# Merged rows of the last branch added by transfers on POOL's queue, their parts one chunk later; T1's product written third

## The chip, the cores and the metric

The kernel runs on one core of one Trainium2 chip. The metric is the device time of one execution in microseconds (us). Of the kernel before, three runs gave a median of 1742.87 us, from 1741.56 to 1743.77. The engines are named as the profile names them: PE multiplies matrices, ACT and DVE work on tiles elementwise, POOL also computes and issues transfers (DMAs), and SP issues transfers only.

## The reference

The kernel computes one layer of an encoder: three token mixers run side by side, each is projected by its own matrix `w_branch`, the three results are gated and summed to `merged`, and `merged` is multiplied by `w_out` and added to x. A feed-forward part follows. The part that matters here, cut from the reference:

```python
branches = jnp.stack([s5_out, diff_out.astype(x.dtype), mem_out.astype(x.dtype)], axis=2)
br = jnp.einsum('blnc,ncd->blnd', branches, w_branch[li])
gates = jax.nn.sigmoid((gl + b_gate[li]).astype(F32)).reshape(Bsz, L, N_BRANCH, D_MODEL)
merged = jnp.sum(gates * br.astype(F32), axis=2).astype(x.dtype)
x = x + merged @ w_out[li]
```

There are 768 tokens in all (256 of one request, 512 of another), and D_MODEL is 1024.

## The kernel before

**Parts.** Every dense product is made of three matmuls (`mm3`, lines 755 to 757): both operands are split into a high part, which is a rounded copy (made by ACT), and a low part, which is the remainder (made by DVE), and hi·hi, hi·lo and lo·hi are added up in one accumulator. So each tile of weights costs ACT one copy and DVE one subtraction before PE can use it.

**Weights.** SP loads raw weights (`wr`, line 539, three buffers of 512 KB). A plain tile becomes `wh` (ACT, line 599) and `wl` (DVE, line 605; in an earlier stage an accumulating transfer of 512 KB, line 603, adds the raw weights onto the negated high part). Each of `wh` and `wl` has four buffers.

**The last branch.** The function `branch7` multiplies the second token mixer's output (n_ = 1) by its 1024 x 1024 matrix in four chunks c of 256 output columns. Each chunk works on two by two blocks, where A are the weights' blocks and B the tokens' blocks, and needs seven products of blocks in place of eight: A11·B11, A12·B21, S2·T2, S1·T1, S3·T3, A22·T4 and S4·B22. S1 to S4 are sums of A blocks, which POOL makes (lines 574, 575, 581 and 583, into `ws`). Their parts, and those of the A blocks, come from lines 557 (ACT, high) and 558 (DVE, low); in the trace a pair is called `wh_A`, `wl_A`, `wh_S` or `wl_S` by the first block in the tile. T1 to T4 are sums of B blocks, made earlier; `ra` holds B11 and B21, `rb` holds B22 and T1, `rc` holds T2 and T3, and `mgd` holds T4. One product is 4 steps of k with three matmuls of 128x384, so 12 matmuls, and a chunk is 84.

**Accumulators.** A11·B11, S2·T2 and S3·T3 add onto one accumulator after another (`brc` in the trace, `chain` in the code), and between them ACT copies its value out: to c11 after the first (line 1683), c12 after the second (line 1685), and c21 after the third (line 1690). S1·T1 has an accumulator of its own (`br`), which is copied to c22 (line 1687) and on which S4·B22 then goes on. A12·B21 and A22·T4 have one each. DVE adds accumulators to c11, c12, c21 and c22 (line 1673). c11 and c12 are the two halves of the first staging tile `bs`, c21 and c22 those of the second. Staging tiles come from a pool of two buffers, so a chunk's first copy into each waits until the chunk before is done with it.

**Merge.** For each of the chunk's two rows m of 128 columns by 768 tokens, POOL loads the gate's logits (`glr`, line 1657, 384 KB, two buffers) and ACT makes the tanh (line 1658). DVE multiplies gate and staging tile in place (line 1677), the row of `merged` is increased by it (line 1678, on POOL for m = 0 and on DVE for m = 1), and ACT and DVE make the sum's high and low part in `mgd` (lines 1679 and 1680). All of this belongs to `merge(m)`.

**After the branch.** `out_rows` multiplies `mgd` by `w_out` (`wo` in the trace) in two halves of four rows, the second half needing rows 4 to 7, and adds x (line 1730). x is loaded by POOL (line 1707) into the buffer that `rc` had.

**Order.** Each engine runs its instructions in a fixed order, which a scheduler sets when the program is built; it may put an instruction ahead of one that the code has earlier, so that chunk 3's A11·B11, for one, stands among chunk 2's products. Engines wait for each other by semaphores, and a waiting instruction holds all behind it on its engine.

Of the kernel before, what the change touches and what calls it, by code (L numbers as in the profile page):

```python
# [8 lines left out]
F32 = mybir.dt.float32  # L9
# [621 lines left out]
def hybrid_block(ctx, tc, A, outs, consts):  # L631
# [866 lines left out]
    with ExitStack() as c5:  # L1498
# [146 lines left out]
        MG = rows_pair("mgd", 0)  # L1645
        RB["T4"] = tuple(t[:, 6:8].rearrange("p a (b t) -> p (a b) t", b=2) for t in MG)

        def branch7(n_):
            for c in range(4):
                w = W.get()  # L1650
# [13 lines left out]
                def prod(l, r, ps=None, start=True):  # L1664
                    if ps is None:
                        ps = psd("br")[:, 0:HT]
                    (wh, wl), (xh, xl) = w[l], RB[r]
                    for k in range(4):
                        mm3(ps, wh[:, k], wl[:, k], xh[:, k], xl[:, k], start and k == 0, k == 3, not start)
                    return ps  # L1670
# [4 lines left out]
                def merge(m):  # L1675
                    M = 2 * c + m
                    v.scalar_tensor_tensor(out=cs[m], in0=gs[m], scalar=1.0, in1=cs[m], op0=add, op1=mul)
                    (v if m else gp).tensor_tensor(out=merged[:, M], in0=merged[:, M], in1=cs[m], op=add)
                    act.activation(MG[0][:, M], merged[:, M], AF.Copy, scale=0.5)
                    v.scalar_tensor_tensor(out=MG[1][:, M], in0=merged[:, M], scalar=0.5,  # L1680
                                           in1=MG[0][:, M].bitcast(F32), op0=mul, op1=sub)

                act.activation(c11, prod("A11", "B11", chain), AF.Copy)
                plus(c11, prod("A12", "B21"))
                act.activation(c12, prod("S2", "T2", chain, False), AF.Copy)
                p5 = prod("S1", "T1")
                act.activation(c22, p5, AF.Copy)
                prod("S3", "T3", chain, False)
                plus(c22, chain)
                act.activation(c21, chain, AF.Copy)  # L1690
                if c < 3:
                    plus(c12, prod("S4", "B22", p5, False))
                    merge(0)
                    plus(c21, prod("A22", "T4"))
                    merge(1)
                else:
                    plus(c21, prod("A22", "T4"))
                    merge(1)
                    plus(c12, prod("S4", "B22", p5, False))
                    merge(0)  # L1700
# [335 lines left out]
```

## Time and profile before

| What | Time |
|---|---|
| Profiled execution | 1743.06 us |
| Its span, first to last instruction | 1741.3 us |
| PE, DVE, ACT, POOL busy in it | 1726.6, 1300.5, 908.6, 302.5 us |
| Last branch's first matmul starts | 1120.74 us after the span's start |
| First matmul of the output product starts | 1183.75 us |

The page of the profile gives the busy time of each engine over the whole span. A timeline gives each instruction's start and duration in us, its engine, its line, what it writes and reads (buffer numbers left out), and in brackets how long the engine stood idle before it and whose instruction ended that. PE's matmuls overlap, so the distance between starts is their pace, and it is shorter than one's duration. The row of a stretch (`a:b`) gives busy times of the engines, and near its end the granted clock of PE, 1.00 being full speed. Rows of transfers give the time that the issue took, and from issue to landing.

### The profile page before, as it was taken

To read this page: it belongs to the slowest core of one execution; us is meant where nothing else is said; L and a number is where in the kernel's file an instruction comes from. 1 tells how busy PE (TensorE), PEld (TensorE's weight loads), DVE (VectorE), ACT (ScalarE), POOL (GpSimd) and SP (SyncE) were. 2 spreads that over 40 slices of the span, in tenths; PEclk is the share of its full clock that TensorE was granted. 3 is DMA by queue.
4 is the path that set the end of the run, shared out by engine and by line. 5 is a ranking of instruction groups with operands and counts; after the bars stand their busy time and mean duration, and the time that the engine had idled before them with its cause. 6 is when DMAs were issued, how large, how long until landed. Compare 5 with 4: busy or idle time off the path is not lost.

```text
span 1741.3 us, 29531 instructions
## 1 busy us (share of the span) xinstructions
PE 1726.6 (99%) x11188; PEld 1608.1 (92%) x11188; DVE 1300.5 (75%) x2405; ACT 908.6 (52%) x1924; POOL 302.5 (17%) x308
## 2 busy tenths in 40 slices
PE   9999999999999999999999999999999999999999
PEld 9999988999999999999989888998889999998887
DVE  7665749699999778887886536685598777776775
ACT  7444543776767346877765434353343333334443
POOL 0000000000000100111000001341036555541130
PEclk9999999999999999999999999999999999999999
DMA  7222636755556454745653435335312323239974
GB/s 268 78 85 91 125 120 135 186 125 143 145 159 159 115 140 103 164 91 156 155 165 117 140 116 157 103 111 174 97 55 91 110 91 109 92 110 295 248 157 97
DMA packets 209213, 234.09 MB, mean 134 GB/s; under 512 B 57832, under 2 KB 173296, under 8 KB 209072
## 3 DMA queue, kind: packets, MB, share of 16 engines
q1 hardware_dynamic: 182160, 167.49, 32.0%
q0 software_dynamic: 17440, 58.34, 15.6%
q10 hardware_dynamic: 9472, 6.39, 1.3%
q8 instruction: 88, 1.44, 0.4%
q14 instruction: 53, 0.43, 0.1%
HBM read 165.78 MB, written 41.22 MB: 119 GB/s over the span
## 4 chain that ended last, share of the span: by engine, by line
PE 95%; DVE 2%; ACT 1%; issue 0%; DMA 0%; POOL 0%; SPq 0%; ACTq 0%; DVEq 0%
PE gl L755 4%; PE gl L756 4%; PE gl L757 4%; PE gate L755 3%; PE gate L756 3%; PE up L756 3%; PE gate L757 3%; PE up L755 3%; PE up L757 3%; PE dn L757 3%; PE dn L755 3%; PE dn L756 3%; PE br L755 3%; PE br L757 3%; PE br L756 3%; PE qk L755 3%
## 5 line engine op out<-in xcount | busy, mean ns | idle before, releaser
L599 ACT ACTIVATE wh<-wr 128x1024 fp32r<-128x1024 f32 x116 | 131.9, 1138 | 52.3 <-PE br L756 13.3
L605 DVE TENSOR_TENSOR wl<-wr,wh 128x1024 fp32r<-128x1024 f32 x74 | 99.2, 1342 | 63.5 <-ACT wh L599 61.7
L755 PE MATMUL gl<-H,wh 128*128 128x256 f32 (+1 forms) x384 | 132.2, 344 | 0.0
L757 PE MATMUL gl<-H,wl 128*128 128x256 f32 (+1 forms) x384 | 129.0, 336 | 0.0
L756 PE MATMUL gl<-H,wh 128*128 128x256 f32 (+1 forms) x384 | 128.7, 335 | 0.0
L603 POOL DMA_DIRECT2D wl<-wr x42 | 36.6, 872 | 483.3 <-ACT wl L602 464.1
L755 PE MATMUL qk<-wh,H 128*128 128x256 f32 x384 | 108.3, 282 | 0.0
L756 PE MATMUL qk<-wl,H 128*128 128x256 f32 x384 | 108.0, 281 | 0.0
L757 PE MATMUL qk<-wh,H 128*128 128x256 f32 x384 | 107.3, 279 | 0.0
L558 DVE TENSOR_TENSOR wl_S<-ws,wh_S 128x512 fp32r<-128x512 f32 x84 | 70.7, 863 | 26.2 <-ACT wh_S L557 26.2
L756 PE MATMUL dn<-wld,dxh 128*128 128x512 f32 x231 | 89.6, 389 | 0.0
L755 PE MATMUL dn<-whd,dxh 128*128 128x512 f32 x231 | 89.5, 389 | 0.0
L757 PE MATMUL dn<-whd,dxl 128*128 128x512 f32 x231 | 88.9, 389 | 0.0
L557 ACT ACTIVATE wh_S<-ws 128x512 fp32r<-128x512 f32 x84 | 49.5, 625 | 73.5 <-PE up L756 36.6
L757 PEld LDWEIGHTS gl<-H,wl 128*128 128x128 f32 x384 | 72.0, 188 | 8.1
L756 PEld LDWEIGHTS gl<-H,wh 128*128 128x128 f32 x384 | 72.2, 188 | 7.2
L755 PEld LDWEIGHTS gl<-H,wh 128*128 128x128 f32 x384 | 72.3, 188 | 6.9
L757 PEld LDWEIGHTS qk<-wh,H 128*128 128x128 f32 x384 | 72.6, 189 | 0.6
L755 PEld LDWEIGHTS qk<-wh,H 128*128 128x128 f32 x384 | 72.4, 188 | 0.6
L756 PEld LDWEIGHTS qk<-wl,H 128*128 128x128 f32 x384 | 72.3, 188 | 0.5
L1296 DVE TENSOR_REDUCE nm<-sc 128x1 f32<-128x512 f32 (+1 forms) x96 | 56.7, 597 | 18.1 <-PE sc L1291 17.2
L1298 ACT ACTIVATE p<-sc,nm 128x512 f32<-128x512 f32 (+1 forms) x96 | 58.8, 615 | 14.4 <-DVE nm L1296 13.9
(535 smaller groups left out, 6076.2 us busy)
## 6 DMA issues: line engine op xcount, KB each, us to landing
wr<-in_w_in_dram SPq DMA_DIRECT2D x48, 512.0 KB, 5.0
wr<-in_w_gate_up_dram SPq DMA_DIRECT2D x44, 512.0 KB, 3.6
wl<-wr POOLq DMA_DIRECT2D x42, 512.0 KB, 5.4
wr<-in_w_branch_dram SPq DMA_DIRECT2D x24, 512.0 KB, 4.5
glr<-gl_scr POOLq DMA_DIRECT2D x24, 384.0 KB, 3.5
hid_scr<-fa SPq DMA_DIRECT2D x11, 768.0 KB, 6.4
wr<-in_w_mem_kv_dram SPq DMA_DIRECT2D x16, 512.0 KB, 4.4
wr<-in_w_in_dram SPq DMA_DIRECT2D x32, 256.0 KB, 3.9
```

Source lines behind the costliest of these rows:

```text
L557: self.nc.scalar.activation(f(hi), src, AF.Copy)
L558: self.nc.vector.tensor_tensor(out=f(lo), in0=src, in1=f(hi).bitcast(F32), op=ALU.subtract)
L599: self.nc.scalar.activation(hi, r, AF.Copy)
L603: self.nc.gpsimd.dma_start(lo, r.bitcast(F32R), accum_op=ALU.add)
L605: self.sub.tensor_tensor(out=lo, in0=r, in1=hi.bitcast(F32), op=ALU.subtract)
L755: pe.matmul(ps, wh, xh, start=start, stop=False, **kw)
L756: pe.matmul(ps, wh, xl, start=False, stop=False, **kw)
L757: pe.matmul(ps, wl, xh, start=False, stop=stop, **kw)
L1296: v.tensor_reduce(out=nm[:, m : m + 1], in_=ps, axis=AX.X, op=ALU.max, negate=True)
L1298: act.activation(pm[:, 0:n], ps, AF.Exp, bias=nm[:, m : m + 1], accum_out=s1s[:, tt : tt + 1] if m == 0 else s2)
```

## The change

In chunks 0 to 2, `merge` no longer adds the gated row with DVE or POOL; a transfer on POOL's queue adds the staging tile to the row of `merged` in memory (line 1684 now). The parts of these rows move into a function of their own (lines 1649 and 1650), which is called in the next chunk, after the copy to c21. In chunk 3 the addition is on DVE for both rows (line 1686), with the parts at once. The product S1·T1 and its copy stand before S2·T2 in the code. The gated product stays on DVE (line 1682), and other lines only shift: 1673 is now 1678, the copies to c11, c22, c12 and c21 are lines 1689, 1692, 1693 and 1696, the gate's two lines are 1662 and 1663, x's load is 1716 and its addition 1739.

```diff
@@ -1645,6 +1645,11 @@
+        def merged_parts(M):
+            act.activation(MG[0][:, M], merged[:, M], AF.Copy, scale=0.5)
+            v.scalar_tensor_tensor(out=MG[1][:, M], in0=merged[:, M], scalar=0.5,
+                                   in1=MG[0][:, M].bitcast(F32), op0=mul, op1=sub)
+
         def branch7(n_):
@@ -1675,19 +1680,23 @@
                 def merge(m):
                     M = 2 * c + m
                     v.scalar_tensor_tensor(out=cs[m], in0=gs[m], scalar=1.0, in1=cs[m], op0=add, op1=mul)
-                    (v if m else gp).tensor_tensor(out=merged[:, M], in0=merged[:, M], in1=cs[m], op=add)
-                    act.activation(MG[0][:, M], merged[:, M], AF.Copy, scale=0.5)
-                    v.scalar_tensor_tensor(out=MG[1][:, M], in0=merged[:, M], scalar=0.5,
-                                           in1=MG[0][:, M].bitcast(F32), op0=mul, op1=sub)
+                    if c < 3:
+                        gp.dma_start(merged[:, M], cs[m], accum_op=add)
+                    else:
+                        v.tensor_tensor(out=merged[:, M], in0=merged[:, M], in1=cs[m], op=add)
+                        merged_parts(M)
 
                 act.activation(c11, prod("A11", "B11", chain), AF.Copy)
                 plus(c11, prod("A12", "B21"))
-                act.activation(c12, prod("S2", "T2", chain, False), AF.Copy)
                 p5 = prod("S1", "T1")
                 act.activation(c22, p5, AF.Copy)
+                act.activation(c12, prod("S2", "T2", chain, False), AF.Copy)
                 prod("S3", "T3", chain, False)
                 plus(c22, chain)
                 act.activation(c21, chain, AF.Copy)
+                if c:
+                    for m in range(2):
+                        merged_parts(2 * c - 2 + m)
                 if c < 3:
                     plus(c12, prod("S4", "B22", p5, False))
                     merge(0)
```

What the scheduler makes of it is shown at three places. First POOL, from the first row's merge of chunk 1 to the last gate load of the branch. Before (`merged<-merged,bs` is the addition, `ws` the weights' sums, `glr` a gate load; numbers tell buffers apart):

```order
L1678 TENSOR_TENSOR merged<-merged,bs_13786 128x768
L574 TENSOR_TENSOR ws_13896<-wr_0_13625,wr_1_13747 128x512
L1657 DMA glr_13923<-gl_scr_152 128x768
L575 TENSOR_TENSOR ws_13897<-ws_13896,wr_0_13625 128x512
L1657 DMA glr_13926<-gl_scr_153 128x768
L583 TENSOR_TENSOR ws_13897<-wr_1_13747,ws_13897 128x512
L581 TENSOR_TENSOR ws_13910<-wr_0_13625 128x512
L1678 TENSOR_TENSOR merged<-merged,bs_13929 128x768
L1657 DMA glr_14047<-gl_scr_154 128x768
L1657 DMA glr_14050<-gl_scr_155 128x768
```

And now, where `DMA merged<-bs` is the accumulating transfer:

```order
L1684 DMA merged<-bs_13782 128x768
L1662 DMA glr_13919<-gl_scr_152 128x768
L574 TENSOR_TENSOR ws_13892<-wr_0_13625,wr_1_13743 128x512
L575 TENSOR_TENSOR ws_13893<-ws_13892,wr_0_13625 128x512
L1684 DMA merged<-bs_13783 128x768
L1662 DMA glr_13922<-gl_scr_153 128x768
L583 TENSOR_TENSOR ws_13893<-wr_1_13743,ws_13893 128x512
L581 TENSOR_TENSOR ws_13906<-wr_0_13625 128x512
L1684 DMA merged<-bs_13925 128x768
L1662 DMA glr_14043<-gl_scr_154 128x768
L1684 DMA merged<-bs_13926 128x768
L1662 DMA glr_14046<-gl_scr_155 128x768
```

Where one addition stood per chunk, two transfers stand now in chunks 1 and 2, each ahead of a gate load; the sums of lines 574 and 575 follow each other with no gate load between, the transfer of chunk 1's second row stands behind them, and chunk 3's addition has left POOL.

Second ACT, from the last weight sum's copy of chunk 3's weights to the second gate of chunk 3. `bs<-brc` and `bs<-br` are the copies of accumulators, `mgd<-merged` the high part of a merged row, line 599 a weight copy for the output product. Before:

```order
L557 ACTIVATE wh_S_13906<-ws_13910 128x512
L599 ACTIVATE wh_0_14035<-wr_0_13778 128x1024
L1690 ACTIVATE bs_13930<-brc_13931 128x384
L1679 ACTIVATE mgd<-merged 128x768
L1683 ACTIVATE bs_14053<-brc_14055 128x384
L1658 ACTIVATE glr_14047<-glr_14047 128x768
L599 ACTIVATE wh_1_14041<-wr_1_13892 128x1024
L1685 ACTIVATE bs_14053<-brc_14055 128x384
L1679 ACTIVATE mgd<-merged 128x768
L1687 ACTIVATE bs_14054<-br_14096 128x384
L1658 ACTIVATE glr_14050<-glr_14050 128x768
```

And now:

```order
L557 ACTIVATE wh_S_13902<-ws_13906 128x512
L599 ACTIVATE wh_0_14031<-wr_0_13774 128x1024
L1696 ACTIVATE bs_13926<-brc_13927 128x384
L1689 ACTIVATE bs_14049<-brc_14051 128x384
L1649 ACTIVATE mgd<-merged 128x768
L1663 ACTIVATE glr_14043<-glr_14043 128x768
L599 ACTIVATE wh_1_14037<-wr_1_13888 128x1024
L1693 ACTIVATE bs_14049<-brc_14051 128x384
L1692 ACTIVATE bs_14050<-br_14079 128x384
L1649 ACTIVATE mgd<-merged 128x768
L1663 ACTIVATE glr_14046<-glr_14046 128x768
```

The high part of chunk 2's first row (before line 1679, now 1649) stood ahead of chunk 3's copy to c11 and now stands behind it; the copy to c22 moves ahead of the second row's high part.

Third PE, in chunk 3, the last four matmuls ahead of S3·T3 and its first two (`br<-mgd` is A22·T4, `brc<-rc,wh_A` S2·T2, `brc<-rc,wh_S` S3·T3). Before:

```order
L757 MATMUL br_14124<-mgd,wl_S_13916 128x384
L755 MATMUL br_14124<-mgd,wh_S_13915 128x384
L756 MATMUL br_14124<-mgd,wh_S_13915 128x384
L757 MATMUL br_14124<-mgd,wl_S_13916 128x384
L755 MATMUL brc_14055<-rc,wh_S_13906 128x384
L756 MATMUL brc_14055<-rc,wh_S_13906 128x384
```

And now:

```order
L757 MATMUL brc_14051<-rc,wl_A_13897 128x384
L755 MATMUL brc_14051<-rc,wh_A_13896 128x384
L756 MATMUL brc_14051<-rc,wh_A_13896 128x384
L757 MATMUL brc_14051<-rc,wl_A_13897 128x384
L755 MATMUL brc_14051<-rc,wh_S_13902 128x384
L756 MATMUL brc_14051<-rc,wh_S_13902 128x384
```

In chunk 3 the products ran S1·T1, S2·T2, A22·T4, S3·T3, S4·B22, and now run S1·T1, A22·T4, S2·T2, S3·T3, S4·B22, so that S3·T3 follows S2·T2 at once on the same accumulator. In the order before, S1·T1 already stood third in all four chunks, ahead of S2·T2.

## The prediction

> **What bounds the kernel now.** I read the page first, then the list of waits of PE (TensorE's matmuls), and then, for the stretch that the change touches, the timeline of each engine.
>
> ```profile
> span 1741.3 us, 29531 instructions
> ...
> PE 1726.6 (99%) x11188; PEld 1608.1 (92%) x11188; DVE 1300.5 (75%) x2405; ACT 908.6 (52%) x1924; POOL 302.5 (17%) x308
> ...
> PEclk9999999999999999999999999999999999999999
> ...
> PE brc L757 <- DVE wl_A L558: 2.1, 1, 2.1
> PE av L1327 <- ACT aT L1315: 1.6, 2, 1.2
> ```
>
> PE is busy for 99% of the span at full granted clock, so this change can win only what PE loses in its own stretch. The second part says where PE waits: its longest wait of the whole run, 2.1 us, is for line 558 on DVE, inside the last branch. The timeline of PE shows the branch from its first matmul to the first of the output product (wo):
>
> ```profile
> 1120.74 0.34 PE L755 MATMUL brc<-ra,wh_A 128*128 128x384 f32 x1
> ...
> 1126.99 0.33 PE L755 MATMUL br<-mgd,wh_A 128*128 128x384 f32 x1
> ...
> 1156.28 0.34 PE L756 MATMUL brc<-ra,wh_A 128*128 128x384 f32 x1
> 1158.74 0.44 PE L757 MATMUL brc<-ra,wl_A 128*128 128x384 f32 x1 [2.12 <-DVE wl_A L558]
> ...
> 1160.17 0.52 PE L755 MATMUL brc<-ra,wh_A 128*128 128x384 f32 x1
> ...
> 1163.36 0.34 PE L756 MATMUL brc<-rc,wh_S 128*128 128x384 f32 x1
> ...
> 1175.12 0.45 PE L755 MATMUL brc<-rc,wh_A 128*128 128x384 f32 x1 [0.33 <-ACT bs L1683]
> ...
> 1183.75 0.39 PE L755 MATMUL wo<-wh,mgd 128*128 128x512 f32 x1
> ```
>
> From 1120.74 to 1126.99 stand 36 matmuls, so one takes 0.1736 us. The branch has 4 chunks of 7 products of 12, 336 matmuls, worth 58.33 us: at that pace it would end at 1179.07. It ends at 1183.75. I call the difference PE's lag; at the end it is 4.68 us, and that is all that can be won. It arises at three places: the wait before 1158.74 (1158.74 less 1156.28 less one pitch, 2.29), ten matmuls 0.32 apart from 1160.17 to 1163.36 (3.19 less 1.74, 1.45), and about 0.5 at 1175.12. The second is the granted clock. In a row by stretch it is the third number from the end, here of this branch, and below it of an earlier stage:
>
> ```profile
> 1160.00:1162.00 2.00, 2.00 (x8) 2.00 (x7) 2.00 (x3) 0.63 (x1) 0.32 (x1) 0.50 0.62 219
> ...
> 905.00:910.00 5.00, 3.58 (x21) 1.00 0.00 0
> ```
>
> After the wait of 2.1 us the clock was 0.50 and the matmuls crept till 1163.36. Between 905 and 910 us PE was idle for 1.42 of 5 us, after a wait of up to 1.2 (L1327), and the clock stayed at 1.00.
>
> What makes the first wait is seen on DVE and POOL:
>
> ```profile
> 1137.84 2.33 DVE L558 TENSOR_TENSOR wl_S<-wr,wh_S 128x512 fp32r<-128x512 f32 x1
> 1141.92 0.95 DVE L1677 SCALAR_TENSOR_TENSOR bs<-glr,bs 128x768 f32<-128x768 f32 x1
> 1155.15 3.54 DVE L558 TENSOR_TENSOR wl_A<-wr,wh_A 128x512 fp32r<-128x512 f32 x2
> 1160.44 0.94 DVE L1677 SCALAR_TENSOR_TENSOR bs<-glr,bs 128x768 f32<-128x768 f32 x1
> 1169.75 0.68 DVE L558 TENSOR_TENSOR wl_S<-ws,wh_S 128x512 fp32r<-128x512 f32 x1
> 1186.04 1.22 DVE L605 TENSOR_TENSOR wl<-wr,wh 128x1024 fp32r<-128x1024 f32 x1
> ...
> 1137.32 2.30 POOL L1678 TENSOR_TENSOR merged<-merged,bs 128x768 f32<-128x768 f32 x1
> 1154.24 2.22 POOL L1678 TENSOR_TENSOR merged<-merged,bs 128x768 f32<-128x768 f32 x1 [2.34 <-DVE bs L1677]
> 1156.42 1.71 POOL L574 TENSOR_TENSOR ws<-wr,wr 128x512 f32<-128x512 f32 x1
> 1158.08 0.55 POOL L1657 DMA_DIRECT2D glr<-gl_scr  x1
> 1158.66 1.30 POOL L575 TENSOR_TENSOR ws<-ws,wr 128x512 f32<-128x512 f32 x1
> ```
>
> An L558 subtraction that nothing disturbs takes 0.68 us (1169.75). The one at 1137.84 began while POOL added merged rows and took 2.33, ending when POOL had ended and 0.55 more had passed; the pair at 1155.15 took 3.54, one ending after POOL's addition, the other after its L574. So an operation of DVE on two SBUF inputs and one of POOL exclude each other here. POOL's addition of 1154.24 costs DVE some 2.2 us, and PE waits for that.
>
> **The change, part by part.** Terms are in lag at the end of the branch; positions are counted in matmuls from 1120.74.
>
> *POOL's and DVE's additions of chunks 0 to 2 go* (three at 2.22 to 2.30 or 1.84 us on POOL, three at 0.95 on DVE), and the scheduler puts the weight work where they were. With DVE's pair of 1155.15 at its undisturbed pace (2 x 0.62) PE finds its weights at matmul 206. The wait of 2.29 goes, the slow clock behind it too: lag there 0 instead of 3.7.
>
> *Six accumulating transfers come in.* Before shows no such transfer from `bs` to `merged`; the nearest are the weight remainders (L603, the first pair of rows), also added into SBUF, and the plain gate loads of 384 KB (L1657, the row between); the last pair is the weight loads:
>
> ```profile
> L603 POOL DMA_DIRECT2D wl<-wr x42: 850/857/1007, 294.7 to 1252.7; - x42
> ...
> DMA to landing us min/median/max: 4.5/5.4/9.5
> ...
> DMA to landing us min/median/max: 3.1/3.4/4.2
> ...
> L539 SPq DMA_DIRECT2D wr<-in_w_branch_dram x3: 367/368/368, 1132.4 to 1151.9; - x3
> ...
> DMA to landing us min/median/max: 3.5/3.7/4.1
> ```
>
> The issue of an L603 holds POOL for 0.86 us, against 2.2 for the addition. Landing, from the start of the issue: at least 3.1 (the fastest gate load, same bytes, but plain), at most 5.4 (the median of L603, which moves 512 KB). L603 undisturbed takes 4.5, and these have 3/4 of its bytes but share the rings with the gate load that follows at once and with weight loads; I take 4.4, nearest to L603. The Trainium skill (DMA: Bandwidth & Descriptors, "Anatomy of one DMA — SWDGE (gpsimd) path") fits a POOL transfer by 2.0 us plus its bytes at 436 GB/s: 2.9 us by estimate for 384 KB. By it the lags below would nearly all vanish; for 512 KB it gives 3.2 where L603 shows 4.5 to 9.5, so I follow the rows.
>
> The transfer still reads `bs` when it is in flight, and the staging tiles have two buffers: a chunk's first copy into `bs` (ACT L1683 and L1687, now L1689 and L1692) waits for the landing of the chunk before. Behind these copies ACT holds the weight splits, and PE's chain products wait for the copies themselves. Before, the same place was:
>
> ```profile
> 1170.93 0.96 DVE L1677 SCALAR_TENSOR_TENSOR bs<-glr,bs 128x768 f32<-128x768 f32 x1
> 1171.97 1.84 POOL L1678 TENSOR_TENSOR merged<-merged,bs 128x768 f32<-128x768 f32 x1 [3.29 <-DVE bs L1677]
> 1173.85 0.85 ACT L1679 ACTIVATE mgd<-merged 128x768 fp32r<-128x768 f32 x1 [0.36 <-POOL merged L1678]
> 1174.60 0.47 ACT L1683 ACTIVATE bs<-brc 128x384 f32<-128x384 f32 x1
> ...
> 1146.46 0.47 ACT L1687 ACTIVATE bs<-br 128x384 f32<-128x384 f32 x1
> ...
> 1147.56 1.14 ACT L557 ACTIVATE wh_S<-ws 128x512 fp32r<-128x512 f32 x2
> ...
> L1673 DVE TENSOR_TENSOR bs<-bs,br x12: 537/542/556, 1127.4 to 1184.7; 128x384 f32<-128x384 f32 x12
> ```
>
> From the gated product (L1677) to the next chunk's first copy went 1.84 + 0.85 + 0.47 us with small gaps: 1170.93 + 0.96 to 1175.07, 3.2. Now it is 4.4 + 0.47 and a signal or two, 5.0. Link by link:
>
> 1. Second row of chunk 0: L1677 started at 1141.92 before, 0.95 long. POOL no longer holds DVE at 1137.84 (2.33 to 0.68), so it ends near 1141.6. Landing 1146.0, copy 1146.5 instead of 1146.93; with the parts (0.75) and the gate (0.75) behind it, ACT's splits start 1147.9 against 1147.56. About even.
> 2. Second row of chunk 1: DVE is ahead, but POOL's two sums L574 and L575 now follow each other without an issue between. L574 needs the weight load issued near 1152.2, which lands 3.7 to 4.1 later, so the sums run 1156.3 to 1159.4, and the gated product behind the second ends at 1160.35 (started 1160.44 before). Landing 1164.75, copy of c22 1165.3. PE's S4·B22 of chunk 2, matmul 246, is due at 1163.45: lag 1.85.
> 3. The same landing frees ACT's part (ends 1166.0), DVE's (0.95), then four weight subtractions of 0.62 with a wait of about 1.3 among them for ACT's split and POOL's L581 (to 1170.8), then two additions (0.47, 0.55): 1171.8. On the last waits S1·T1 of chunk 3, since its accumulator is the one S4·B22 used: matmul 276, due 1168.65, lag 3.1. Two matmuls of S4·B22 now stand behind S3·T3; they end before 1170, ahead of DVE.
> 4. A22·T4 (matmul 288, due 1170.74) waits for the accumulator that DVE frees after the gated product (0.95), a weight remainder (1.14, the pitch of 1186.04) and an addition (0.55): 1174.4, lag 3.65.
> 5. First row of chunk 2: gated product 1171.8 to 1172.75, landing 1177.15, copy 1177.65. S2·T2 of chunk 3 is matmul 300 now, due 1172.82: lag 4.9. A22·T4 ahead of it covers 2.08 us, which is already in the count.
> 6. S3·T3 follows S2·T2 at once in chunk 3 and adds onto the same accumulator, so it waits for the copy of c12: 0.33 for the last matmul, some 0.75 left of the weight copy ahead of it on ACT (1.05), 0.47. Another 1.5: lag 6.4. Before, A22·T4 stood between and covered it.
>
> So 6.4 against 4.68: +1.7. The weight loads share the rings with the new transfers; if the load of link 2 takes 4.1 to 4.5, links 2 to 6 move by up to 0.8; I add 0.5. Sum: +2.2.
>
> *T1's product third*: the order of before already has it third in all four chunks, so the rewritten line alone gives 0; what moves is A22·T4 of chunk 3 (links 5 and 6).
>
> *The last chunk's additions both on DVE, its order of products, and the x loads:*
>
> ```profile
> 1189.91 2.67 DVE L1680 SCALAR_TENSOR_TENSOR mgd<-merged,mgd 128x768 fp32r<-128x768 f32 x2 [0.91 <-ACT mgd L1679]
> ...
> 1197.59 0.69 DVE L1730 TENSOR_TENSOR x<-x,wo 128x512 f32<-128x512 f32 x1 [5.01 <-PE wo L757]
> ```
>
> The output product first needs the last two rows' parts in its second half, and x after that. The parts end at 1192.58 before and near 1194 now; PE reaches that half 52 matmuls in, near 1196 before and 1198 now: 0, covered by 4 us. The loads of x, behind POOL's addition till 1190.65, move up to about 1183.5; first used at 1197.59, behind PE: 0.
>
> **Sum.** The profiled execution took 1743.06 us (span 1741.3), 0.19 above the median 1742.87 of the three runs. 1743.06 + 2.2 = 1745.3.
>
> **The rivals.**
>
> *Short landing.* Three landings lie in series (links 1, 2 and 5). If the transfers land like the fastest gate load, in 3.1, that is 3 x 1.3 less: lag 3.0 with the loads' 0.5, so 1741.4, and 1740.9 if the loads are not disturbed. For it speaks the size; against it every L603. Chance 0.14. By the Trainium skill's fit (same page and section) the same sum comes to 1740.8, an estimate.
>
> *Long landing: slower.* ACT's queue becomes the bound. The place is the copies behind links 1, 2 and 5; a landing of 4.85 decides, from where three times the excess (0.45) carries the change past +3.5. At the median of L603, 5.4, lag is 6.9 + 3.0: 1748.3. For it speaks that median, which is what such transfers took with loads beside them; against it 3/4 of the bytes. Chance 0.30.
>
> *The clock drops again.* The new waits are 0.5 to 1.9 us each, between the 1.2 that left the clock at 1.00 and the 2.12 that halved it. If the one of link 2 halves it for 3.3 us, at most 1.45 is added: 1746.7. The Trainium skill (TensorE: Matmul & The Clock Gate, Part 1, the HAM clock gate) lets the clock drop after an idle window of about 3.4 us, and by that rule nothing is added; the trace has it drop after 2.12 us of waiting. Chance 0.10, counted as slower.
>
> *Faster by more than 3.5* would need landings shorter than any shown and link 6 hidden too: 0.04.
>
> **How the numbers follow.** A measurement here can tell about 0.2%, 3.5 us, from no change: 1739.4 to 1746.4. My forecast, 3.7 to 4.85 us of landing, has 0.42 and lies within; short landing lies within as well. Faster 0.04, same 0.56, slower 0.40. The forecast's own range is 1743.2 to 1746.6. The range for 8 in 10 runs from the short landing (1740.9) to one of 5.4 with a slow clock (1748.3 + 1.45, 1749.8).
>
> **What the profile of after would show.** Right: no wait at the third matmul of chunk 3's first product; landings of 4 to 5 us for `merged<-bs`; PE's waits named to ACT's copies into `bs` (S4·B22 of chunk 2, S2·T2 and S3·T3 of chunk 3) and to DVE's addition before chunk 3's T1 product; ACT idle until a transfer ahead of L1689 and L1692; the first wo matmul near 1186. Wrong: landings outside 3.1 to 5.4, PE still waiting for an L558, or PE's waits gone while the branch ends as late.

## The result: slower by 0.26%, within the range

The changed kernel took 1746.89 us (median of 10 runs, 1745.27 to 1749.84) against 1742.83 of the kernel before in its 10 runs beside it: a ratio of 1.0026, with a 95% interval of 1.0016 to 1.0036, or 4.06 us more. The prediction said 1745.3 in a range of 1740.9 to 1749.8. The time lies within that range, but 0.3 us above the forecast's own narrower range (1743.2 to 1746.6) and above 1746.4, up to which the prediction counted a time as no change.

The page of the changed kernel's profile, its first lines:

```profile
span 1744.9 us, 29543 instructions
PE 1725.3 (99%) x11188; PEld 1605.8 (92%) x11188; DVE 1294.9 (74%) x2403; ACT 909.1 (52%) x1924; POOL 298.8 (17%) x310
```

PE is busy about as long as before (1726.6 us then) and DVE 5.6 us less; what grew is PE's waiting. The list of PE's waits (line waited for, total us, times, longest):

```profile
PE brc L755 <- ACT bs L1689: 2.7, 2, 1.8
PE brc L755 <- ACT bs L1693: 2.3, 1, 2.3
...
PE br L755 <- ACT bs L1692: 1.2, 1, 1.2
PE br L755 <- DVE bs L1678: 1.1, 2, 0.9
```

The wait for line 558 is gone, and six waits in its own stretch stand in its place, all for ACT's copies out of accumulators and for DVE's additions behind them. PE's timeline shows where:

```profile
1118.54 0.34 PE L755 MATMUL brc<-ra,wh_A 128*128 128x384 f32 x1
...
1157.42 0.44 PE L755 MATMUL brc<-rc,wh_S 128*128 128x384 f32 x1 [0.91 <-ACT bs L1689]
...
1163.74 0.44 PE L755 MATMUL br<-rb,wh_S 128*128 128x384 f32 x1 [1.16 <-ACT bs L1692]
...
1170.12 0.44 PE L755 MATMUL br<-rb,wh_S 128*128 128x384 f32 x1 [0.91 <-DVE bs L1678]
...
1172.71 0.45 PE L755 MATMUL br<-mgd,wh_S 128*128 128x384 f32 x1 [0.23 <-DVE bs L1678]
...
1176.92 0.44 PE L755 MATMUL brc<-rc,wh_A 128*128 128x384 f32 x1 [1.83 <-ACT bs L1689]
...
1181.54 0.44 PE L755 MATMUL brc<-rc,wh_S 128*128 128x384 f32 x1 [2.26 <-ACT bs L1693]
...
1187.38 0.39 PE L755 MATMUL wo<-wh,mgd 128*128 128x512 f32 x1
```

The branch now takes 1187.38 - 1118.54 = 68.84 us against 63.01 before, so the lag at its end (over 336 matmuls at 0.1736, 58.33 us) is 10.51 against 4.68: 5.83 us more. The span grew by 3.6 only, since the branch began 2.20 us earlier in this execution. In the profiles shown below the branch, whose code ahead is the same in all of them, begins anywhere from 1118.5 to 1121.6, so that part is taken as the difference of one execution from another; from the branch's end to the end of the span it is 557.5 us in both. The lag tells more than the span of one profile, and the medians of the runs decide on the time.

Why the copies come late is seen in chunk 3. The group of the accumulating transfers, whose last line is the least, median and greatest us from issue to landing:

```profile
L1684 POOL DMA_DIRECT2D merged<-bs x6: 865/878/908, 1135.2 to 1174.0; - x6
...
DMA to landing us min/median/max: 4.3/4.8/7.1
```

The same line of the group of this branch's gate loads:

```profile
DMA to landing us min/median/max: 3.4/5.2/7.6
```

POOL's timeline, the issues of chunk 2's transfers and chunk 3's first gate load:

```profile
1171.36 0.88 POOL L1684 DMA_DIRECT2D merged<-bs  x1 [3.98 <-DVE bs L1682]
1171.95 0.87 POOL L1662 DMA_DIRECT2D glr<-gl_scr  x1
1173.95 0.86 POOL L1684 DMA_DIRECT2D merged<-bs  x1 [1.14 <-DVE bs L1682]
```

And ACT's timeline:

```profile
1176.38 0.49 ACT L1689 ACTIVATE bs<-brc 128x384 f32<-128x384 f32 x1 [6.25 <-DMA merged<-bs]
...
1179.32 0.84 ACT L1663 ACTIVATE glr<-glr 128x768 f32<-128x768 f32 x1 [1.72 <-DMA glr<-gl_scr]
1180.07 1.04 ACT L599 ACTIVATE wh<-wr 128x1024 fp32r<-128x1024 f32 x1
1181.01 0.47 ACT L1693 ACTIVATE bs<-brc 128x384 f32<-128x384 f32 x1
```

The first row's transfer of chunk 2 is issued at 1171.36; ACT's copy to c11 waits for its landing till 1176.38, 6.25 us idle. The gate load issued right behind it, at 1171.95, lands at 1179.3; before the change gate loads took 3.1 to 4.2. ACT's tanh (L1663) waits for it another 1.72, a weight copy follows, and only then the copy to c12 (L1693), for which S3·T3 waits. After that wait of 2.26 the clock dropped. Of the rows by stretch, the last shows it (0.57, the third number from the end). The two ahead of it show how full the 16 DMA engines were (the second number from the end, 1 being all busy; in these rows it comes out a little above 1 at times):

```profile
1176.00:1178.00 2.00, 1.08 (x6) 1.00 0.99 355
1178.00:1180.00 2.00, 1.27 (x8) 1.00 1.10 246
...
1182.00:1184.00 2.00, 2.00 (x9) 0.57 0.13 35
```

### The profile page after: what moved, and what is told of

It reads as the page before. It is cut to its first block, busy times and chain, and to the rows that moved or that the text cites. A ratio compares the mean times of both kernels' runs of the same rounds, so it can differ in the third digit from the quotient of the medians.

```text
span 1744.9 us, 29543 instructions
## 1 busy us (share of the span) xinstructions
PE 1725.3 (99%) x11188; PEld 1605.8 (92%) x11188; DVE 1294.9 (74%) x2403; ACT 909.1 (52%) x1924; POOL 298.8 (17%) x310
## 4 chain that ended last, share of the span: by engine, by line
PE 96%; DVE 1%; ACT 1%; DMA 1%; issue 0%; SPq 0%; POOL 0%; ACTq 0%
PE gl L755 4%; PE gl L757 4%; PE gl L756 4%; PE gate L755 3%; PE gate L757 3%; PE gate L756 3%; PE up L757 3%; PE up L756 3%; PE up L755 3%; PE br L756 3%; PE dn L757 3%; PE br L757 3%; PE br L755 3%; PE dn L755 3%; PE dn L756 3%; PE qk L756 3%
```

## The experiments

In the kernels below, unless said otherwise, each engine's order in the branch is pinned row by row to that of the kernel named, by an order-only edge between neighbours, since the scheduler would answer any edit with an order of its own. So an edit shows alone. Only t1_alone stands as the scheduler built it. Each ratio is against runs of the kernel before made beside that kernel; their medians lay between 1741.93 and 1742.83, so rows compare better by ratio than by median. The lags are of one profiled execution each. The numbers of all:

| Kernel | Additions of chunks 0 to 2 | Lag at branch's end, us | Median, us | Ratio to before, 95% interval |
|---|---|---|---|---|
| before | POOL and DVE | 4.68 | 1742.83 | |
| t1_alone | POOL and DVE | 4.98 | 1743.24 | 1.0004 (0.9994 to 1.0013) |
| before_dve | DVE | 2.36 | 1739.85 | 0.9986 (0.9977 to 0.9995) |
| late_parts_dve | DVE | 3.68 | 1740.83 | 0.9991 (0.9982 to 1.0000) |
| dve_order_back | DVE | 1.15 | 1738.59 | 0.9981 (0.9972 to 0.9990) |
| changed kernel | transfers | 10.51 | 1746.89 | 1.0026 (1.0016 to 1.0036) |
| plain_transfer | transfers that don't add | 3.45 | 1740.93 | 0.9997 (0.9987 to 1.0008) |
| gate_first | transfers | 17.07 | 1754.39 | 1.0073 (1.0055 to 1.0092) |
| chunk3_order_back | transfers | 9.57 | 1748.28 | 1.0037 (1.0025 to 1.0049) |
| c12_copy_first | transfers | 9.47 | 1746.36 | 1.0029 (1.0018 to 1.0039) |
| staging_apart | transfers | 8.75 | 1749.44 | 1.0035 (1.0022 to 1.0047) |
| staging_apart_2 | transfers | 11.05 | 1748.87 | 1.0036 (1.0024 to 1.0048) |
| transfers_covered | transfers | 7.01 | 1744.49 | 1.0015 (1.0006 to 1.0023) |
| gates_on_sp | transfers | 6.72 | 1746.78 | 1.0022 (1.0013 to 1.0031) |

### The product with T1 third, alone

```diff
                 plus(c11, prod("A12", "B21"))
-                act.activation(c12, prod("S2", "T2", chain, False), AF.Copy)
                 p5 = prod("S1", "T1")
                 act.activation(c22, p5, AF.Copy)
+                act.activation(c12, prod("S2", "T2", chain, False), AF.Copy)
```

> The kernel before with one edit of the change: the product S1·T1 and its copy written ahead of S2·T2. The built order of every engine is that of the kernel before, row by row. Theory (this edit is worth nothing): the time stays within 0.2% of before (1739.4 to 1746.4 us), and the branch, from its first matmul to the first of the output product, takes 63.0 us again (before: 1183.75 less 1120.74), with the wait for line 558 and the slow clock at the same place. Rival (the order of the code still matters somewhere, or the branch's length differs from profile to profile by as much as the change's +5.8 us): a branch of 61 or of 66 us or more.

The time of t1_alone is that of before (1.0004), the branch took 63.31 us. The scheduler had the product third already, and this edit does nothing. PE's timeline, the two longest waits of the branch:

```profile
1159.41 0.44 PE L757 MATMUL brc<-ra,wl_A 128*128 128x384 f32 x1 [1.90 <-DVE wl_A L558]
...
1176.35 0.44 PE L755 MATMUL brc<-rc,wh_A 128*128 128x384 f32 x1 [1.77 <-ACT bs L1683]
```

The lag is nearly the same (4.98 against 4.68), but it is made up in another way. Here the clock held after a wait of 1.90, and PE reached S2·T2 of chunk 3 with a lag of 2.8 instead of 3.9; there it waited 1.77 instead of 0.33 for the copy to c11. So in the kernel before, the slow clock was not the only bound: in these two executions S2·T2 of chunk 3 starts 54.4 us (before) and 54.7 us (t1_alone) after the branch's first matmul, with the slow clock or without it, since the chain of DVE, POOL and ACT that ends in that copy comes out at nearly the same time.

### The transfers replaced, their orders kept

```diff
                     if c < 3:
-                        gp.dma_start(merged[:, M], cs[m], accum_op=add)
+                        v.tensor_tensor(out=merged[:, M], in0=merged[:, M], in1=cs[m], op=add)
                     else:
```

> The changed kernel without its transfers, all other orders held: the six additions of chunks 0 to 2 are made by DVE (0.95 us each) right behind the gated product; the parts stay one chunk later. Theory A (the transfers cost the time): staging tiles come free 1 us after the gated product instead of 4.8; the lag is 2 to 5, the time 1739 to 1743, not slower than before. Theory B (the parts made late and the order that the scheduler built around them cost the time): lag above 8, time above 1745.

Theory A holds for this kernel (late_parts_dve): lag 3.68, 1740.83 us. With the same order and the same late parts, but without the transfers, the time is 1746.89 - 1740.83 = 6 us lower (ratios 1.0026 and 0.9991) and no longer above before. Two waits over 0.4 us are left on PE's timeline:

```profile
1171.40 0.44 PE L755 MATMUL br<-mgd,wh_S 128*128 128x384 f32 x1 [1.22 <-DVE bs L1678]
...
1177.24 0.44 PE L755 MATMUL brc<-rc,wh_S 128*128 128x384 f32 x1 [1.40 <-ACT bs L1693]
```

The next kernel, plain_transfer, tells whether it is the transfer or the adding in it:

```diff
                     if c < 3:
-                        gp.dma_start(merged[:, M], cs[m], accum_op=add)
+                        gp.dma_start(merged[:, M], cs[m])
                     else:
```

> The changed kernel with all orders held, but the six transfers copy the staging tile over the row of merged instead of adding it (so the sum over branches is left out in chunks 0 to 2). Theory A (the adding makes the landing long): they land in 3.1 to 3.5 us after the issue like the plain gate loads, three landings in series give back 3 x 1.3 us and the clock does not drop: lag 4 to 6.5. Theory B (384 KB from SBUF to SBUF takes that long in any case): landing 4.3 to 4.9 as with the addition, lag 9 to 11.

The group of the plain transfers:

```profile
DMA to landing us min/median/max: 2.6/3.0/5.2
```

And the longest wait of PE that is left, in chunk 3:

```profile
1177.38 0.44 PE L755 MATMUL brc<-rc,wh_S 128*128 128x384 f32 x1 [1.99 <-ACT bs L1693]
```

They land in 3.0 us (median) instead of 4.8, and the lag is 3.45, a little below theory A's 4 to 6.5. Of the 10.51 us of lag, 7.06 go with the adding, which makes the landing 1.8 us longer. That is more than three landings in series (5.4), since the slow clock goes too (1.57) and the gate loads land sooner (4.3 in the median of all loads of the branch, 5.2 with adding). Of these the clock may be luck: it held here after a wait of 1.99, and in c12_copy_first below it dropped after one of 1.91.

### Around the landing: buffers, orders, queues

First, other staging tiles for every second chunk (line numbers from 1666 on are 4 higher in this kernel, staging_apart, and in transfers_covered and gates_on_sp below):

```diff
-        t4 = t4p.tile([128, 4, HT], F32, name="t4")
+        t4 = t4p.tile([128, 4, HT], F32, name="t4", tag="t4")
...
-                cs = [stg.tile([128, TOK], F32, name=uid("bs"), tag="brr") for _ in range(2)]
+                if c % 2:
+                    cs = t4p.tile([128, 2, TOK], F32, name=uid("bs"), tag="t4")
+                    cs = [cs[:, 0], cs[:, 1]]
+                else:
+                    cs = [stg.tile([128, TOK], F32, name=uid("bs"), tag="brr") for _ in range(2)]
```

> The changed kernel, every engine's order held as it is, but chunks 1 and 3 take their two staging tiles from another buffer (that of T4's raw sums, free by then), so that no copy into a staging tile waits for the landing of the chunk just before. Theory A (the landings hold the copies, and the copies hold PE): the waits of PE for L1689 and L1692 (0.91, 1.16 and 1.83 us in the changed kernel) go, and with them what follows of them; of the lag of 10.5 us at the branch's end (68.84 less 58.33) 2 to 6 is left, and the time falls by 4 to 8 us to 1739 to 1743. Theory B (the parts made one chunk later, the new order and the traffic hold PE, whatever buffer is used): the lag stays above 8.5 and the time within 2 us of the changed kernel's 1746.9.

> The kernel of staging_apart again, since its profile (lag 8.75, 1.8 less than the changed kernel's) and its times (median 1749.4 of five) don't fit together. If the median was by chance of few runs: 1744 to 1747 now and a lag of 7 to 10. If the profiled execution was the odd one: a lag of 11 or more and times near 1749 again.

The copies to c11 and c22 no longer wait for a landing, and yet nothing is won: 1.0035 and 1.0036. The first profiled execution was the fastest of its runs (1745.42 of 1745.42 to 1749.71), so its lag of 8.75 is the odd one. In the second, with a lag of 11.05, the clock dropped twice, the first time after a wait of 2.16 us. Theory B holds: both lags are above 8.5, and by ratio the times are some 1.6 us above the changed kernel's. ACT's timeline in chunk 3 of that first execution:

```profile
1169.29 0.48 ACT L1693 ACTIVATE bs<-brc 128x384 f32<-128x384 f32 x1
1175.77 0.84 ACT L1649 ACTIVATE mgd<-merged 128x768 fp32r<-128x768 f32 x1 [5.99 <-DMA merged<-bs]
1178.27 0.84 ACT L1663 ACTIVATE glr<-glr 128x768 f32<-128x768 f32 x1 [1.66 <-DMA glr<-gl_scr]
1179.02 1.04 ACT L599 ACTIVATE wh<-wr 128x1024 fp32r<-128x1024 f32 x1
1179.96 0.47 ACT L1697 ACTIVATE bs<-brc 128x384 f32<-128x384 f32 x1
```

The copy to c11 (L1693 here) is made at 1169.29, seven us earlier than in the changed kernel. But the next in ACT's order is the high part of the merged row (L1649), which needs the sum and so the landing, and then the tanh, which needs the gate load. The copy to c12 (L1697) stands behind both, and S3·T3 waited 4.06 us for it (4.14 in the second profile). Freeing the buffer moved the wait to the next instruction in the same queue.

Then two edits of order in the changed kernel. In PE's order of chunk3_order_back the twelve matmuls of S2·T2 move ahead of A22·T4's (the first of each shown):

```
+L755 MATMUL brc_1508_14051<-rc_12989,wh55_A12_13896 128x384
...
 L755 MATMUL br_1511_14124<-mgd_13595,wh55_S4_13911 128x384
...
-L755 MATMUL brc_1508_14051<-rc_12989,wh55_A12_13896 128x384
```

> The changed kernel with one thing moved on PE, all other orders held: in chunk 3 A22·T4 stands between S2·T2 and S3·T3 again, as before the change. Theory A (what follows the landing only moves; the landing sets the end): S2·T2 comes 2.08 us earlier and waits that much longer, 1.83 + 2.08 = 3.9 us, for the same copy at 1176.9; behind it A22·T4 covers the copy of c12, so the wait of 2.26 before S3·T3 shrinks to about 0.3 or goes. The sum is even up to the clock, which drops after the wait of 3.9 instead of that of 2.26: lag 9 to 10.8 against 10.5, time within 1.7 us of 1746.9. Theory B (S3·T3 right behind S2·T2 is what costs, link 6 of the prediction): 2.4 of waiting and 1.6 of slow clock are won, lag near 6.5, time near 1743.

PE's timeline, S2·T2's first matmul in chunk 3:

```profile
1178.64 0.58 PE L755 MATMUL brc<-rc,wh_A 128*128 128x384 f32 x1 [4.51 <-ACT bs L1689]
```

The wait before S2·T2 grew to 4.51, those before A22·T4 and S3·T3 are gone, and the clock dropped after it: lag 9.57 and 1.0037, theory A. In c12_copy_first one row moves in ACT's order of the changed kernel:

```
 L1689 ACTIVATE bs_1506_14049<-brc_1508_14051 128x384
 L1649 ACTIVATE mgd_13595<-merged_11575 128x768
+L1693 ACTIVATE bs_1506_14049<-brc_1508_14051 128x384
 L1663 ACTIVATE glr_1504_14043<-glr_1504_14043 128x768
 L599 ACTIVATE wh56_1_14037<-wr56_1_13888 128x1024
-L1693 ACTIVATE bs_1506_14049<-brc_1508_14051 128x384
```

> The changed kernel with one row of ACT's order moved, all other orders of the branch held: chunk 3's copy to c12 (L1693) stands ahead of the gate's tanh (L1663) and the weight copy (L599) that were ahead of it. In the changed kernel that tanh waited 1.72 us for a gate load that was issued behind the accumulating transfer and landed 7 us after its issue, and S3·T3 waited 2.26 us for the copy behind it, after which the clock dropped. Theory A (the gate load's late landing, through ACT's queue, makes the last wait and the slow clock): S3·T3 waits 0.7 to 0.9 instead of 2.26, the clock stays at 1.00, lag at the branch's end 7.0 to 7.6 instead of 10.5, time 3 us under the changed kernel's 1746.9. Theory B (the copy of c12 waits for S2·T2 itself or PE is held elsewhere as long): lag stays above 9.5.

PE's timeline, S2·T2's first matmul and S3·T3's:

```profile
1177.24 0.45 PE L755 MATMUL brc<-rc,wh_A 128*128 128x384 f32 x1 [1.91 <-ACT bs L1689]
...
1181.63 0.45 PE L755 MATMUL brc<-rc,wh_S 128*128 128x384 f32 x1 [0.58 <-ACT bs L1693]
```

The row of the stretch between them, with the clock at 0.50:

```profile
1178.00:1180.00 2.00, 2.00 (x8) 0.50 1.06 255
```

S3·T3 waits 0.58 now, a little less than theory A said, but the clock dropped one product sooner, after a wait of 1.91 that had been 1.83, and the output product waited 0.36 for ACT. Lag 9.47 and 1.0029: of the 2.44 that the wait had cost, about 1 us is left as a gain in lag, none in time. So theory A is right about the wait (the gate load's late landing reached S3·T3 through ACT's queue) and wrong about what it would win: the lag it gave was 7.0 to 7.6, the time 3 us lower.

In gate_first POOL's order changes, each gate load ahead of the transfer that it followed:

```
+L1662 DMA glr_1504_14043<-gl_scr14_154 128x768
 L1684 DMA merged_11575<-bs_1498_13925 128x768
-L1662 DMA glr_1504_14043<-gl_scr14_154 128x768
```

> The changed kernel with POOL's order changed alone: each gate load is issued ahead of the accumulating transfer that it followed, 0.57 us apart. Theory A (POOL's queue moves one after the other, so whichever is issued second lands some 2.5 to 3 us after the first): gate loads land 3.2 to 3.9 us after their issue as without transfers, transfers 6 to 7 after theirs, and as the staging copies wait for the transfers the lag grows to 11.5 to 14. Theory B (both share the rings): transfers still land in 4.3 to 5.2 us, gate loads in 4 to 5.2, lag 8 to 11.

The group of the transfers:

```profile
DMA to landing us min/median/max: 5.6/6.3/7.8
```

And that of the gate loads:

```profile
DMA to landing us min/median/max: 3.3/4.3/6.4
```

The transfers now take 6.3 us instead of 4.8, the gate loads 4.3 instead of 5.2 in the median: what is issued second pays. The lag is 17.07, beyond even theory A's 14, and both of its two runs (1754.01 and 1754.77) are far above the changed kernel's. But the gate loads did not come down to the 3.4 of before, so the two also share, as theory B has it.

Last, in transfers_covered, everything that was seen to wait was moved: staging apart, chunk 3's order of before on PE, and on ACT and DVE the parts and the tanh behind the copies and weight parts that PE needs. Of ACT's order in chunk 3:

```
 L1693 ACTIVATE bs_14048<-brc_14049 128x384
-L1649 ACTIVATE mgd<-merged 128x768
-L1663 ACTIVATE glr_14042<-glr_14042 128x768
 L599 ACTIVATE wh_1_14036<-wr_1_13887 128x1024
 L1697 ACTIVATE bs_14048<-brc_14049 128x384
 L1696 ACTIVATE bs_14048<-br_14077 128x384
+L1649 ACTIVATE mgd<-merged 128x768
+L1663 ACTIVATE glr_14042<-glr_14042 128x768
```

> The transfers kept, all that was seen to wait for them moved away: staging tiles of chunks 1 and 3 apart (as in staging_apart), A22·T4 of chunk 3 between S2·T2 and S3·T3 again, and on ACT and DVE the parts of merged rows and the gate's tanh, which wait for landings, behind the copies of accumulators and the weight parts that PE waits for (chunk 2's second row; chunk 3's first). POOL's and SP's orders as in the changed kernel. Theory A (a landing costs only by what is queued behind it, so 4.8 us of it can be hidden): waits of PE below 1 us each, lag at the branch's end 0.1 to 2.5, time 1737.5 to 1740.5. Theory B (the gate loads, late behind the transfers on POOL's queue, hold the gated products and so the staging tiles and accumulators anyhow): lag above 5, time above 1743.

PE's two waits, in its timeline:

```profile
1170.92 0.44 PE L755 MATMUL br<-rb,wh_S 128*128 128x384 f32 x1 [2.70 <-DVE bs L1682]
...
1185.54 0.50 PE L755 MATMUL wo<-wh,mgd 128*128 128x512 f32 x1 [3.93 <-ACT bs L1700]
```

And the list of ACT's waits within the branch (total us, times, longest):

```profile
ACT glr L1663 <- DMA glr<-gl_scr: 9.5, 7, 3.3
ACT mgd L1649 <- DMA merged<-bs: 7.3, 4, 2.4
```

Lag 7.01, 1.0015 (1.0006 to 1.0023): by ratio 0.11% better than the changed kernel, with intervals that overlap, and still slower than before. ACT's tanh waited 3.3 for chunk 2's second gate load, with weight copies behind it and DVE behind those (the first wait), and in chunk 3 the copy to c21 (L1700) stood behind two gate loads and a landing (the second, ahead of the output product). That the gate loads are to blame was the next theory; in gates_on_sp the loads are issued by SP:

```diff
-                    gp.dma_start(g, gl_scr[8 * n_ + 2 * c + m])
+                    nc.sync.dma_start(g, gl_scr[8 * n_ + 2 * c + m])
```

> The kernel of transfers_covered (lag 7.01, two waits of PE: 2.70 for DVE before chunk 3's T1 product, 3.93 for ACT before the output product; ACT waited 9.5 us for gate loads) with one thing changed: the gate loads of this branch are issued by SP, between the weight loads, so that on POOL's queue the accumulating transfers are alone; all other orders held. Theory A (gate loads behind the transfers on one queue are what still held ACT): gate loads land 3 to 4 us after issue, transfers in 4.2 to 4.5, both waits of PE fall below 1 us, lag 0.1 to 2.5, time 1737.5 to 1740.5, faster than before. Theory B (landings of weights and gates get late by the traffic whatever the queue, or ACT waits for the landings of the transfers themselves): lag above 5, time above 1743.

The group of the transfers:

```profile
DMA to landing us min/median/max: 4.5/6.0/8.6
```

That of the gate loads, now on SP:

```profile
DMA to landing us min/median/max: 3.2/4.1/4.8
```

PE's first matmul of the output product, and the row of a later stretch:

```profile
1184.70 0.80 PE L755 MATMUL wo<-wh,mgd 128*128 128x512 f32 x1 [4.74 <-ACT bs L1700]
...
1186.00:1188.00 2.00, 2.00 (x6) 0.50 1.03 418
```

On ACT's timeline the part that waits for the transfer of chunk 2's second row, which POOL issued at 1173.12:

```profile
1181.75 0.84 ACT L1649 ACTIVATE mgd<-merged 128x768 fp32r<-128x768 f32 x1 [3.46 <-DMA merged<-bs]
```

Two stretches (second number from the end: share of the DMA engines):

```profile
1176.00:1178.00 2.00, 2.00 (x13) 1.00 0.97 308
1178.00:1180.00 2.00, 1.96 (x12) 1.00 1.05 274
```

And the same stretches of late_parts_dve:

```profile
1176.00:1178.00 2.00, 0.76 (x4) 1.00 0.01 3
1178.00:1180.00 2.00, 2.00 (x14) 1.00 0.25 67
```

Theory A fell, and theory B holds (lag 6.72, 1746.78 us): the gate loads come in 4.1, but the transfers now need 6.0, the last one 8.6, and ACT waits for them instead. In both kernels the DMA engines are nearly all busy from 1176 to 1180 (0.97 and 1.05 here, 0.99 and 1.10 in the changed kernel, against 0.01 and 0.25 without transfers). Here the loads of x also started earlier, at 1178, and fall into the same stretch, so how much of the 8.6 us is theirs and how much the gate loads' stays open.

In these last two kernels the lag at the branch's end is not all that was lost. After the waits of 3.93 and 4.74 the clock was at half inside the output product (till 1190.7 in gates_on_sp), and from that product's first matmul to the end of the span it is 559.3 and 560.5 us, against 557.5 to 557.6 in all the other profiles: 1.8 and 3.0 us more. That goes most of the way to explain why gates_on_sp, with a lag of 6.72, is as slow as the changed kernel.

### Without transfers: what is best

In before_dve DVE makes POOL's additions:

```diff
-                    (v if m else gp).tensor_tensor(out=merged[:, M], in0=merged[:, M], in1=cs[m], op=add)
+                    v.tensor_tensor(out=merged[:, M], in0=merged[:, M], in1=cs[m], op=add)
```

> The kernel before with POOL's four additions made by DVE in the same place (right behind the gated product), parts at once, every other order held. Theory A (POOL's addition beside DVE's subtractions was the loss of before, and 0.95 us more of DVE per chunk is nearly all hidden): the wait of 2.12 at the first chain product of chunk 3 falls to 0.3 to 1.2, no slow clock, lag 1.5 to 3, time 1738.5 to 1741. Theory B (DVE is then late itself; the parts had to be moved a chunk later to gain anything): lag 4 or more, time as before.

Theory A: 0.9986, lag 2.36, all by taking POOL's additions to DVE in the kernel before; the wait for line 558 is down to 0.97. Late parts in themselves (late_parts_dve, lag 3.68) are no better than that. What spoils them is chunk 3's order, as the last kernel, dve_order_back, shows: late_parts_dve with S2·T2's twelve matmuls ahead of A22·T4's.

> The kernel of late_parts_dve (DVE makes the additions of chunks 0 to 2, parts one chunk later, no transfers; lag 3.68) with one thing moved on PE: in chunk 3 A22·T4 stands between S2·T2 and S3·T3 again. Theory A (both waits that late_parts_dve has left, 1.22 before A22·T4 for DVE and 1.40 before S3·T3 for the copy of c12, come of the new place of A22·T4): S2·T2 is ready when its turn comes, A22·T4 comes 2.1 later and finds its accumulator free, and covers the copy; lag 0.3 to 1.2, time 1737.5 to 1739.5, faster than before by 0.2 to 0.3%. Theory B (S2·T2 then waits for its own copy, c11, as long): lag 2.5 to 4, time as late_parts_dve, 1740.8.

PE's timeline: the wait that is left, S2·T2's first matmul of chunk 3, and the first of the output product:

```profile
1156.49 0.44 PE L757 MATMUL brc<-ra,wl_A 128*128 128x384 f32 x1 [0.36 <-DVE wl_A L558]
...
1171.15 0.44 PE L755 MATMUL brc<-rc,wh_A 128*128 128x384 f32 x1
...
1179.73 0.50 PE L755 MATMUL wo<-wh,mgd 128*128 128x512 f32 x1
```

Theory A again: one wait of 0.36 is left in the branch, the lag is 1.15, and 1738.59 us is below both kernels: 0.9981 of before (0.9972 to 0.9990). The same move on PE that gained nothing with the transfers (chunk3_order_back) gains 2.5 us of lag here, since the copy to c11 is on time. In time the gain is less sure: 0.9981 against 0.9991, with intervals that overlap.

## Why the prediction was right, and where it was off

- *The wait for line 558 goes.* Right: no wait stands at matmul 206, and the lag there is 0 in the changed kernel.
- *Landing.* 4.4 was taken; measured from 4.3 up, 4.8 in the median, 4.9 for chunk 2's first row and 7.1 for its second. The last lies outside the 3.1 to 5.4 whose leaving the prediction called a sign of being wrong, but the copy that needed it came later in any case. The direction from which the estimate came was right (nearest to the other accumulating transfers, though 3/4 of their bytes), the value 0.4 short. The median stayed just under 4.85, the landing from which the prediction counted on a slower kernel, and yet the medians moved by 4.06 us, over its 3.5: the rest came from link 6 and the clock, below. So the likeliest case, no change (0.56), did not come; slower, which did, had 0.40.
- *Short landing* as a rival: plain_transfer is that case on the chip, with its landing of 3.0 against the 3.1 assumed. Lag 3.45 against 3.0, time 1740.93 beside 1741.93 for before in the same session, which is no clear change; the sum of that rival came out near. Its terms fit less well: 2.2 of the 3.45 arise at S3·T3, where 1.5 were counted. The Trainium skill's fit (DMA: Bandwidth & Descriptors, "Anatomy of one DMA — SWDGE (gpsimd) path"), 2.9 us by estimate, agrees with plain_transfer's 3.0. It doesn't hold for the transfers that add, at 4.8.
- *Link 1* (about even): right, no wait there.
- *A link was missed ahead of link 2.* The first row's transfer of chunk 1, issued 1152.13, landed at 1156.9, and S2·T2 of chunk 2 (matmul 218) waited 0.91 for the copy to c11 that waited for it. Lag after it 1.14. It shortens the wait at link 2 by as much, so it is inside the lag measured there.
- *Links 2 to 5.* Lag after them predicted 1.85, 3.1, 3.65 and 4.9; measured 2.60, 3.77, 4.28 and 6.41. Every one stands at the named place, with the named releaser (L1692, L1678, L1678, L1689). The excess of 0.6 to 0.75 begins with link 2's landing and grows to 1.5 with the landing of link 5.
- *Link 6.* Predicted 1.5 for S3·T3 behind S2·T2, measured 2.53 (8.94 less 6.41). In late_parts_dve, without transfers, the same place costs 1.6. The mis-sized term: on ACT ahead of the copy stood not only a weight copy but the tanh, whose gate load was late behind the transfer (1.72 idle). The working let the transfers suffer from the gate loads and the weight loads, but not the gate loads from the transfers. With the copy moved ahead of the tanh (c12_copy_first) that wait was 0.58.
- *The clock.* Given a chance of 0.10, it happened: 1.57 us (10.51 less 8.94), from 1182.3 to 1185.7, after the wait of 2.26 and not after that of link 2. By the Trainium skill's rule (TensorE: Matmul & The Clock Gate, Part 1, an idle window of about 3.4 us) nothing would have been added here, and this trace differs from it: 2.26 us of waiting were enough.
- *The sum.* Lag 10.51 instead of 6.9: 1.0 more by link 5 (6.41 against 4.9 and the 0.5 added for the loads), 1.0 more at link 6, 1.57 of clock. (The three places into which the prediction split the lag of before, 2.29, 1.45 and 0.5, make 4.24 of its 4.68; the rest is single slower matmuls, such as the first behind each wait.) So the branch grew by 5.83 in this execution, while the medians grew by 4.06. That the remaining 1.8 is the spread of single executions is argued, not shown; the two profiles of staging_apart differ by 2.3 in lag. So that the median came within 1.6 us of the forecast, while the lag missed it by 3.6, is in part luck.
- *"T1's product third" gives 0*: right (t1_alone). *Additions of the last chunk, x loads*: 0, right; from the output product to the end both profiles take 557.5 us.
- *All that can be won is 4.68*: dve_order_back wins 3.5 of it in lag and 3.3 us in time, without the transfers.

## What to carry to other kernels

An addition taken off an engine and made by a transfer isn't free: the source tile stays taken, and the sum unknown, until the landing, so ask for every in-order queue what stands behind the first instruction that needs either. Count also what the transfer does to the loads that are issued behind it, since their landing holds other queues. And when an edit is meant to relieve one engine, measure the plain alternative: here the same additions made by DVE, 0.95 us each, won 0.14% (before_dve), where the transfers lost 0.26%.

## What the runs showed of the hardware

- A transfer within SBUF that adds took 4.8 us (median) from issue to landing for 384 KB, and one that copies 3.0, same queue, same tiles, same order; the issue held POOL for 0.88 and 0.55 us.
- The clock does not follow the length of PE's last wait alone. It dropped after waits of 1.91 (c12_copy_first), 2.12 (before), 2.16 (staging_apart_2) and 2.26 (the changed kernel), and held after 1.90 (t1_alone), 1.99 (plain_transfer), 2.34 (gate_first) and 2.70 (transfers_covered). Each spell at half lasted 3.4 us, or twice that (6.8 us in gates_on_sp and at the second drop of staging_apart_2, which began 13.66 us, four times 3.415, after the first).
- Where a wait falls seems to decide. Cut a trace with a spell into stretches of 3.41 us, counted back and forth from the spell's start. The stretch just before each spell holds 1.91 to 3.41 us of waiting by PE's timeline (1.91 in c12_copy_first, 1.98 and 2.16 in staging_apart_2, 2.12 in before, 2.26 in the changed kernel). No spell began after a stretch with less, and the most among those is 1.78 (c12_copy_first): the 2.34 of gate_first is split into 1.56 and 0.78, the 2.70 of transfers_covered into 1.10 and 1.60. One case doesn't fit: in gates_on_sp the spell went on for a second 3.4 us with 0.79 of waiting in its first. In t1_alone and plain_transfer there is no spell to count from, so their 1.90 and 1.99 stay open. This is read from the traces afterwards; no run was made to test it.
- A drop of the clock can be free: in t1_alone it didn't happen and the branch was no shorter (63.31 us, 63.01 in before with the drop), since a later wait grew from 0.33 to 1.77.
